# Gate and up of two feed-forward parts by seven block products, with low weight halves added by DMA

## The chip, the cores and the metric

The kernel runs on one core of one Trainium2 chip. The metric is device time of one execution in microseconds (us). The engines are called as in the profile: PE (TensorE matmul), PEld (its weight loads), DVE (VectorE), ACT (ScalarE), POOL (GpSimd) and SP (SyncE, which here issues DMAs only). PEclk in a row is the granted TensorE clock; 1.00 is the upper of its two levels, 2.4 GHz.

## What is computed

One inference step of a hybrid decoder layer for 512 prompt tokens and 32 sample tokens (544 columns, 1024 features): a half-step feed-forward part, a mixer (attention and a gated delta rule), a merge, a second half-step feed-forward part, a last norm. All data are float32. The change is in the two feed-forward parts and in how weights are prepared outside the mixer.

```
def _swiglu(x, w_gu, w_down):
    gate, up = jnp.split(x @ w_gu, 2, axis=-1)
    return (jax.nn.silu(gate) * up) @ w_down

x = x + 0.5 * _swiglu(_rms(x, norm_ffn1), w_ffn1_gu, w_ffn1_down)
h = _rms(x, norm_mix)
...                                   # mixer: h @ w_in, attention, delta rule
x = x + merged.astype(x.dtype) @ w_out
x = x + 0.5 * _swiglu(_rms(x, norm_ffn2), w_ffn2_gu, w_ffn2_down)
```

D_MODEL is 1024 and D_FF is 2816, so each part has 22 tiles of 128 gate and 128 up columns (44 in both parts), and a down projection of 22 x 8 weight tiles.

## The kernel before

**Layout and numbers.** Activations stand with features on the partitions, as tiles of 128 x 544, worked on in two halves h of 272 tokens. The kernel keeps float32 precision by splitting every operand into a high part hi (rounded to the matmul's float32r type) and a rest lo. A product of one weight tile with one half of the tokens is three matmuls of 128x128 by 128x272: hi with hi, hi with lo, lo with hi (`unit`). A unit of work over 8 weight tiles is so 24 matmuls into one PSUM bank.

**Order.** `make_plan` writes a list of units, and `kernel_units` goes through it: it brings in weights for the unit (`prefetch`), issues its matmuls, and issues what empties its bank (`evac`) one or more units later. Every engine works through its own instructions in that order. In a feed-forward part the units are, for 11 column tiles, gate and up for both halves (`u_g`, `u_u`: 4 units, 96 matmuls for a tile), then 16 down units over these 11 tiles (`u_d`), and the same again. The mixer in the middle has side chains that a meter interleaves; its order is the same on every engine before and after the change.

**Weights.** They come as chunks of 8 tiles (128 x 1024, 512 KB) by plain DMAs from SP (from POOL in the mixer) into a few raw buffers. `split_next` takes a group of 4 tiles: ACT copies it as hi into a G tile, then DVE (in the mixer POOL) writes raw - hi as lo. 12 G tiles are held in the feed-forward parts, and a look-ahead of 4 groups is kept (LA). A chunk's buffer takes its next load when both of its groups are split.

**Around them.** `xw_tile` makes hi and lo of x * w_norm; the 1/rms of the tokens (`R(h)`) is multiplied in when gate and up leave PSUM. PSUM has 8 banks: 3 called mm and 5 called sd. Nearly all instructions carry line 120 (131 after), where the meter calls the engine, so the rows are read by their tile names: xh, xl (x as hi and lo), hh (gated activations), G (weights as hi and lo), raw, r (1/rms), acc (sums of squares), H (scratch of 272 columns).

Of the kernel before, what the change touches and what calls it, by code (L numbers as in the profile page):

```python
# [25 lines left out]
FB = 11  # L26
# [11 lines left out]
CFG = dict(S=62, S2=4, G=4, G2=8, RAW=2, U3=3, H=10, HM=6, LA=4, LAG=3.0, SLACK=0.0, BANKS=3, PRE=3, LOV=("pa", "pb"), CV=0, WARM=4, EP=8, DUE=2, RES=0, RQ="gpsimd")  # L38


# [85 lines left out]
class Plan:  # L126
    """Order in which the 128 x 128 weight tiles are used; host and chip follow it."""
# [16 lines left out]
def stagger(n, tail, head=0):  # L144
    """(tile, half) order: the first `head` and the last `tail` tiles go half by half."""
    out = [(i, h) for h in range(2) for i in range(head)]
    for i in range(head, n - tail):
        out += [(i, 0), (i, 1)]
    out += [(i, h) for h in range(2) for i in range(n - tail, n)]
    return out  # L150


def make_plan():
    pl = Plan()
    units = []

    def ffn(which):
        gu, dn = f"w_ffn{which}_gu", f"w_ffn{which}_down"
        for b in range(2):
            order = stagger(FB, 0, 2 if b == 0 else 0) if (which, b) != (1, 0) else stagger(FB, 2, 2)  # L160
            for f, h in order:
                f += b * FB
                units.append(("g", which, f, h, pl.col(gu, range(KT), f * P)))
                units.append(("u", which, f, h, pl.col(gu, range(KT), (FT + f) * P)))
            for n, h in stagger(KT, 0 if b == 0 else 2 if which == 1 else 4):
                units.append(("d", which, b, n, h, pl.col(dn, range(b * FB, b * FB + FB), n * P)))

# [36 lines left out]
def consts():  # L204
    """Arrays that depend on shapes alone: identity, masks and distances."""
# [53 lines left out]
class Builder:  # L259
    def __init__(self, tc, nc, A, pl, units, cp, sp, pp, dp):  # L260
# [5 lines left out]
        self.next_group = 0  # L266
        self.next_raw = self.top = 0
        self.side = []
        self.due, self.rings = {}, {}
        self.last = False  # L270
        self.busy = set()
        self.nps = 0
        self.in_mix = False
        self.plan_groups()
# [15 lines left out]
    def until(self, ok):  # L290
        """The side chains go on until something holds."""
# [26 lines left out]
    def S2(self, i, shape=(P, NT), dt=F32, name="s2"):  # L318
        return self.T(shape, dt, "S2", CFG["S2"], name) if i < CFG["S2"] else self.S(shape, dt, name)

    def ring(self, tag, bufs, t):
        """A tile waits for the one whose place it takes."""
# [26 lines left out]
    def mm_ps(self):  # L349
        self.nps += 1  # L350
        if not self.in_mix and self.nps % 8 > 2:
            return self.sd_ps()
# [28 lines left out]
    def mm(self, out, lhsT, rhs, start=True, stop=True):  # L381
        return self.nc.tensor.matmul(out, lhsT, rhs, start=start, stop=stop)
# [5 lines left out]
    def rsqrt(self, out, v, tmp, steps):  # L388
        """out = v ** -0.5 by a shifted exponent and Newton steps."""
# [3 lines left out]
        for k in range(steps):  # L393
            a, b = (-0.703952253, 0.703952253 * 2.38924456) if k == 0 else (-0.5, 1.5)
            self.tt(tmp, out, out, ALU.mult)
            self.stt(tmp, tmp, a, v, ALU.mult, ALU.mult)
            self.stt(out, tmp, b, out, ALU.add, ALU.mult)
            yield "vector"

# [1 line left out]
    def load_raw(self, upto):  # L401
        nch = self.A["in_W_dram"].shape[0]
        while self.next_raw <= min(upto, nch - 1):
            c = self.next_raw
            pool, tag, bufs = self.sp, "raw", CFG["RAW"]
            if c % 3 == 2 and not self.in_mix and c * CHUNK // GRP not in self.resident:
                pool, tag, bufs = self.mp, "raw2", 1
# [5 lines left out]
    def plan_groups(self):  # L413
        self.last_use, self.resident = {}, set()
        first_pa = next(i for i, u in enumerate(self.units) if u[0] == "pa")
        first_ba = next(i for i, u in enumerate(self.units) if u[0] == "ba")
        for i, u in enumerate(self.units):
            for t in u[-1]:
                self.last_use[t // GRP] = i
                if first_ba <= i < first_pa:  # L420
                    self.resident.add(t // GRP)
        self.held = {"G": [], "G2": []}

    def split_next(self, ui, pool=None):
        """Bring the next group of weight tiles in as hi + lo if a slot is free."""
        k = self.next_group
        c = k * GRP // CHUNK
        for tag, bufs in (("G2", CFG["G2"]), ("G", CFG["G"])):
            if tag == "G2" and (k in self.resident or self.in_mix):
                continue  # L430
# [3 lines left out]
        else:  # L434
            return False
        self.held[tag].append(k)
        self.load_raw(c)
        o = (k * GRP % CHUNK) * P
        src = self.raws[c][:, o:o + GRP * P]
# [210 lines left out]
    def kernel_units(self):  # L650
# [4 lines left out]
        for ui, u in enumerate(self.units):  # L655
# [8 lines left out]
            for e in pend[:n]:  # L664
                e()
# [1128 lines left out]
```

## Time and profile before

| what | value |
|---|---|
| time, median of 3 runs | 1730.75 us (1727.0 to 1732.26) |
| span of the profiled execution | 1730.2 us |
| PE busy | 1656.1 us, 96% |
| DVE, ACT, POOL busy | 62%, 33%, 22% |
| DMA, mean over the span | 119 GB/s |

The profiled execution's span lies inside the three measured times; what lies around the span is no more than the spread of the runs. How to read the rows: the page's first part gives busy time by engine; its fourth part follows back what released the last work; the windows give the same busy times for one stretch, with the number of instructions, and the groups give the mean time of one instruction of a kind.

### The profile page before, as it was taken

How to read it: one execution, taken by the hardware profiler on the slowest of the kernel's cores; microseconds unless marked ns; L12 is line 12 of the kernel's file. 1: busy time of each engine (PE TensorE's matmuls, PEld its weight loads, DVE VectorE, ACT ScalarE, POOL GpSimd, SP SyncE). 2: the span in 40 equal slices, each digit the busy share in tenths (PEclk: the TensorE clock that was granted, in tenths of full speed). 3: DMA queues.
4: the chain of work that ended last, by engine and by line, in shares of the span. 5: the costliest groups of instructions: out<-in, count | busy, mean ns of one | idle time of the engine just before them, and what ended most of it. 6: DMA issues, size and time to landing. Idle time of an engine off the chain costs nothing.

```text
span 1730.2 us, 33573 instructions
## 1 busy us (share of the span) xinstructions
PE 1656.1 (96%) x13373; PEld 1607.8 (93%) x13373; DVE 1072.3 (62%) x2508; ACT 573.1 (33%) x1356; POOL 373.4 (22%) x441
## 2 busy tenths in 40 slices
PE   8999999999988999999899899999999999999997
PEld 7999999999988888888889788999999999999996
DVE  7754255545879869789958665344456654255534
ACT  5332223332332324343333244333233323223332
POOL 5000000011545534454425233420011000000012
PEclk9999999999999999999999999999999999999999
DMA  5223222322333455446347666332243222223221
GB/s 177 87 85 98 86 86 86 98 85 75 111 100 115 135 180 185 135 156 193 117 137 238 171 219 182 123 119 89 86 139 97 84 89 87 97 74 98 86 75 63
DMA packets 116434, 205.13 MB, mean 119 GB/s; under 512 B 30962, under 2 KB 57108, under 8 KB 116276
## 3 DMA queue, kind: packets, MB, share of 16 engines
q1 hardware_dynamic: 104708, 162.43, 29.2%
q0 software_dynamic: 10992, 39.99, 7.7%
q8 instruction: 105, 1.72, 0.4%
q10 hardware_dynamic: 576, 0.56, 0.1%
q14 instruction: 53, 0.43, 0.1%
HBM read 172.20 MB, written 30.73 MB: 117 GB/s over the span
## 4 chain that ended last, share of the span: by engine, by line
PE 73%; DVE 20%; DMA 3%; ACT 2%; issue 2%; SPq 1%; POOL 0%; DVEq 0%; ACTq 0%
PE sd L120 40%; PE mm L120 32%; DVE y L120 4%; DVE Yc L120 3%; DVE inv L120 2%; DVE H L120 1%; DVE nrm L120 1%; DVE ast L120 1%; DVE av L120 1%; DVE s L120 1%; DVE R L120 1%; DMA md<-ast 1%; DVE U L120 1%; DVE kq L120 1%; DVE r L120 1%
## 5 line engine op out<-in xcount | busy, mean ns | idle before, releaser
L120 PE MATMUL mm<-xh,G 128*128 128x272 f32 x3632 | 753.7, 297 | 21.6 <-DVE smp L120 10.4
L120 PEld LDWEIGHTS mm<-xh,G 128*128 128x128 f32 x3632 | 596.6, 192 | 42.5 <-issue 26.5
L120 PE MATMUL mm<-xl,G 128*128 128x272 f32 x1816 | 530.0, 292 | 0.5 <-DVE xl L120 0.4
L120 PE MATMUL sd<-xh,G 128*128 128x272 f32 x1904 | 363.4, 288 | 0.0
L120 PEld LDWEIGHTS mm<-xl,G 128*128 128x128 f32 x1816 | 349.2, 192 | 1.4 <-DVE xl L120 0.6
L120 ACT ACTIVATE G<-raw 128x512 fp32r<-128x512 f32 x474 | 273.3, 619 | 178.6 <-PE mm L120 111.6
L120 PEld LDWEIGHTS sd<-xh,G 128*128 128x128 f32 x1904 | 300.5, 188 | 0.2
L120 POOL TENSOR_TENSOR G<-raw,G 128x512 fp32r<-128x512 f32 x158 | 217.3, 1391 | 322.7 <-ACT G L120 303.0
L120 PE MATMUL sd<-xl,G 128*128 128x272 f32 x952 | 273.8, 288 | 0.0
L120 DVE TENSOR_TENSOR G<-raw,G 128x512 fp32r<-128x512 f32 x316 | 204.7, 690 | 70.9 <-ACT G L120 66.7
L120 POOL TENSOR_TENSOR acc<-acc,H 128x272 f32<-128x272 f32 x55 | 44.7, 814 | 911.5 <-ACT H L120 908.1
L120 PEld LDWEIGHTS sd<-xl,G 128*128 128x128 f32 x952 | 179.0, 188 | 0.1
L120 PE MATMUL sd<-hh,G 128*128 128x272 f32 x1287 | 163.0, 288 | 0.0
L120 PEld LDWEIGHTS sd<-hh,G 128*128 128x128 f32 x1287 | 161.8, 188 | 0.1
L120 ACT ACTIVATE H<-H 128x272 f32<-128x272 f32 (+1 forms) x105 | 45.1, 429 | 193.4 <-DVE H L120 193.4
L120 ACT ACTIVATE hh<-H 128x272 fp32r<-128x272 f32 x88 | 38.0, 431 | 202.0 <-DVE H L120 202.0
L120 PE MATMUL mm<-hh,G 128*128 128x272 f32 x825 | 104.7, 288 | 0.0
L120 PEld LDWEIGHTS mm<-hh,G 128*128 128x128 f32 x825 | 103.8, 188 | 0.0
L120 DVE SCALAR_TENSOR_TENSOR y<-U,vec,y 128x568 f32<-128x568 f32 x72 | 94.2, 1308 | 7.8 <-ACT y L120 6.0
L120 DVE SCALAR_TENSOR_TENSOR H<-H,H 128x272 f32<-128x272 f32 x120 | 55.2, 460 | 26.3 <-ACT H L120 25.8
L120 DVE SCALAR_TENSOR_TENSOR x<-sd,x 128x272 f32<-128x272 f32 x49 | 21.4, 439 | 77.9 <-PE sd L120 77.9
L120 DVE TENSOR_TENSOR hh<-H,hh 128x272 fp32r<-128x272 f32 x88 | 38.9, 442 | 43.8 <-ACT hh L120 43.8
(257 smaller groups left out, 1853.3 us busy)
## 6 DMA issues: line engine op xcount, KB each, us to landing
raw<-in_W_dram SPq DMA_DIRECT2D x161, 512.0 KB, 3.6
raw<-in_W_dram POOLq DMA_DIRECT2D x76, 512.0 KB, 4.0
qkv<-qd SPq DMA_DIRECT2D x36, 256.0 KB, 5.4
st<-in_ssm_dram SPq DMA_DIRECT2D x32, 256.0 KB, 4.5
cache<-in_kc_dram SPq DMA_DIRECT2D x28, 256.0 KB, 5.2
cache<-in_vc_dram SPq DMA_DIRECT2D x28, 256.0 KB, 4.3
qd<-av SPq DMA_DIRECT2D x24, 256.0 KB, 4.2
out_dram<-av SPq DMA_DIRECT2D x24, 256.0 KB, 3.8
```

The lines of the kernel that those rows point to most:

```text
L120: r = f(*args, **kw)
```

## The change

**Seven products.** For the last 15 of 22 column tiles in the first part and the last 16 in the second, gate and up of both halves are computed as one 2 x 2 block product: gate and up by lower and upper half of the features (4 weight tiles each), times these halves by the two halves of the tokens. Seven products of 4 weight tiles each (12 matmuls) stand in place of 8 (the table PROD). Products 1 and 2 and 4 use weights as they are (A11, A12, A22), the others use sums of weight groups (S1 to S4), which `sums` makes on DVE (on POOL for the first 3 tiles of each part) from the raw chunks into 6 new buffers sw. The activations' block sums (T1 to T4) are made once for each part by `tset`, during the last plain tiles. The first 7 and 6 column tiles stay as they were.

**Seeds.** A tile uses three banks A, B, C. B starts as a copy of -A that ACT writes into PSUM after product 1, and products 6, 7 and 4 are summed onto it. A matmul with a zero matrix (float32, 272 columns) opens the first five B banks of each part.

**Low weights.** Outside the mixer, from unit 6 on, a plain group's lo is no longer written by DVE: ACT writes -hi beside hi, and POOL issues a DMA that reads the same 256 KB again from DRAM and adds them onto -hi. lo of the sums S1 to S4 stays on DVE.

**Sizes.** 4 raw buffers (2 shared, 2 of the phase) and 11 G tiles, look-ahead 8 groups and at most 2 new groups for a unit; 3 blocks of 8, 7 and 7 column tiles instead of 2 of 11; the last 4 down tiles of both parts go half by half; the first x tiles are loaded after four raw chunks instead of one.

In the built program PE has 372 fewer matmuls of 272 columns and 10 with the zero matrix more. The core of the diff:

```diff
-CFG = dict(S=62, S2=4, G=4, G2=8, RAW=2, U3=3, H=10, HM=6, LA=4, ..., EP=8, DUE=2, RES=0, RQ="gpsimd")
+CFG = dict(S=62, G=4, G2=7, SW=6, RAW=2, RAW2=2, U3=3, H=7, HM=6, LA=4, LF=8, LS=5, EP=6, ..., DUE=3, RES=0, RQ="gpsimd")
+PROD = {1: ("A11", "B11", "A", True), 2: ("A12", "B21", "A", False), 6: ("S2", "T2", "B", False), 7: ("S3", "T3", "B", False),
+        4: ("A22", "T4", "B", False), 5: ("S1", "T1", "C", True), 3: ("S4", "B22", "C", False)}
+FBS = (8, 7, 7)
+NC = {1: 7, 2: 6}
+EARLY = 3
+TS = {1: (-20, -16, -12, -8), 2: (-18, -15, -11, -7)}
...
+        for b, n in enumerate(FBS):
+            for f in range(max(f0, nc), f0 + n + 1):
+                if f < FT:
+                    w(f, *[p for p in (1, 5) if (f, p) not in begun])
+                if f > nc and (f - 1, 3) not in begun:
+                    w(f - 1, 3)
+                if f < FT and (f, 6) not in begun:
+                    w(f, 6)
+                if f > nc and (f - 1, 4) not in begun:
+                    w(f - 1, 4)
+                if f < FT and (f, 2) not in begun:
+                    w(f, 2, 7)
+            for m, h in stagger(KT, 0 if b < 2 else 4):
+                units.append(("d", which, b, m, h, pl.col(dn, range(f0, f0 + n), m * P)))
+            f0 += n
...
+    def sums(self, j):
+        k = self.jobs[j] if j < len(self.jobs) else ()
+        if not k or k[0] == "g" or k in self.sw or self.in_mix or not self.have(k):
+            return
+        kind, gx, gy = k
+        eng = self.nc.gpsimd if gx in self.early else None
...
+        if kind == "S1":
+            self.tt(new("S1"), self.raw(gy), self.raw(gy + 1), ALU.add, eng)
...
+            self.tt(new("S2"), self.sw["S1", gx, gy], self.raw(gx), ALU.add, eng)
...
+            self.tt(new("S3"), self.raw(gx), self.raw(gy + 1), ALU.add, eng)
+            self.tt(new("S4"), self.raw(gx + 1), self.sw["S2", gx, gy], ALU.add, eng)
+        self.read_raw(k)
+        self.load_raws()
...
         self.act(t[:, 0, :], src, AF.Copy)
-        self.tt(t[:, 1, :], src, t[:, 0, :], ALU.subtract, self.nc.gpsimd if pool else None)
+        if raw and not self.in_mix and ui >= CFG["EP"]:
+            self.act(t[:, 1, :], t[:, 0, :], AF.Copy, scale=-1.0)
+            self.read_raw(k)
+            self.load_raws()
+            self.nc.gpsimd.dma_start(t[:, 1, :], self.A["in_W_dram"][...][:, o:o + GRP * P], accum_op=ALU.add)
...
-        load_x(0, range(4))
-        self.load_raw(0)
-        load_x(0, range(4, KT))
+        load_x(0, range(4))
+        self.load_raws()
+        load_x(0, range(4, KT))
...
+    def u_w(self, which, f, p, wids):
+        wn, bn, bank, start = PROD[p]
+        if start:
+            self.bank[f, bank] = self.mm_ps(bank)[:, :NH]
+        ps = self.bank[f, bank]
+        hi, lo = self.w(wids[0])
+        for j in range(4):
+            c = slice(j * P, j * P + P)
+            xh, xl = self.ts_bs[bn, j, 0], self.ts_bs[bn, j, 1]
+            self.mm(ps, hi[:, c], xh, start and j == 0, False, True)
+            self.mm(ps, hi[:, c], xl, False, False, True)
+            self.mm(ps, lo[:, c], xh, False, j == 3 and last, True)
...
+            if p == 1:
+                b = self.bank[f, "B"] = self.mm_ps("B")[:, :NH]
+                if self.nb < 5:
+                    self.mm(b, self.zero, self.x[0][:, h0], True, True, True)
+                self.act(b, ps, AF.Copy, scale=-1.0)
+            elif p == 6:
+                self.act(e["V"], ps, AF.Copy)
+            elif p == 5:
+                self.act(e["p5"], ps, AF.Copy)
+            elif p == 2:
+                self.act(e["t"][:, h0], ps, AF.Tanh, scale=0.5)
+            elif p == 7:
+                self.tt(e["u"], ps, e.pop("p5"), ALU.subtract)
+                self.stt(t, t, 1.0, self.bank.pop((f, "A")), ALU.add, ALU.mult)
+            elif p == 3:
+                self.tt(g, ps, g, ALU.subtract)
+                self.act(t, g, AF.Tanh, scale=0.5)
+                self.stt(t, t, 1.0, g, ALU.add, ALU.mult)
+                self.tt(t, t, e.pop("u"), ALU.mult)
+            else:
+                self.tt(t[:, h0], t[:, h0], ps, ALU.mult)
+                self.split(*self.h[f], t)
```

ACT in the first part, at one column tile, before. hh is a gated activation's hi, H is its tanh, G<-raw a weight group's hi:

```order
L120 ACTIVATE hh_216_1547<-H_211_1511 128x272
L120 ACTIVATE G_218_1554<-raw_198_1384 128x512
L120 ACTIVATE G_219_1557<-raw_198_1384 128x512
L120 ACTIVATE H_223_1588<-H_222_1587 128x272
L120 ACTIVATE G_224_1591<-raw_208_1483 128x512
L120 ACTIVATE G_225_1594<-raw_208_1483 128x512
L120 ACTIVATE hh_228_1624<-H_223_1588 128x272
L120 ACTIVATE H_232_1657<-H_231_1656 128x272
```

ACT in the first part, among the tiles with seven products, after. t<-mm is product 2's tanh, sd<-mm is the seed of B, H<-sd the copy of product 5, G<-sw a sum's hi, G<-G a -hi:

```order
L131 ACTIVATE hh_389_2630<-t_370_2509 128x544
L131 ACTIVATE G_391_2635<-raw_363_2454 128x512
L131 ACTIVATE G_391_2635<-G_391_2635 128x512
L131 ACTIVATE t_392_2651<-mm_372_2513 128x272
L131 ACTIVATE G_393_2653<-sw_383_2591 128x512
L131 ACTIVATE G_398_2676<-sw_375_2532 128x512
L131 ACTIVATE sd_400_2691<-mm_394_2655 128x272
L131 ACTIVATE G_401_2694<-sw_387_2613 128x512
L131 ACTIVATE H_402_2708<-sd_399_2678 128x272
L131 ACTIVATE G_403_2711<-raw_360_2430 128x512
L131 ACTIVATE G_403_2711<-G_403_2711 128x512
L131 ACTIVATE t_392_2651<-H_386_2611 128x272
```

Where four group copies stood for a column tile there are now ten copies of 512 columns and six of 272 or 544; the next chunk, raw_404, takes the buffer of raw_360, so SP issues it behind the copy G_403<-raw_360.

DVE in the first part, at one column tile, before. G<-raw is a group's lo, r is 1/rms:

```order
L120 TENSOR_TENSOR G_293_2434<-raw_279_2247,G_293_2434 128x512
L120 TENSOR_TENSOR G_294_2437<-raw_279_2247,G_294_2437 128x512
L120 SCALAR_TENSOR_TENSOR H_292_2431<-H_292_2431,H_291_2430 128x272
L120 TENSOR_TENSOR H_292_2431<-H_292_2431,r_73_361 128x272
L120 TENSOR_TENSOR H_292_2431<-H_292_2431,mm_296_2442 128x272
L120 TENSOR_TENSOR hh_298_2468<-H_292_2431,hh_297_2467 128x272
```

DVE in the first part, among the tiles with seven products, after, around the sum that reads raw_404 (S1, then S2); t<-t,sd is the multiplication by product 4's bank that the next hh waits for:

```order
L131 TENSOR_TENSOR sw_396_2672<-raw_363_2454,raw_382_2572 128x512
L131 TENSOR_TENSOR sw_397_2674<-raw_363_2454,sw_387_2613 128x512
L131 TENSOR_TENSOR G_398_2676<-sw_375_2532,G_398_2676 128x512
L131 TENSOR_TENSOR G_401_2694<-sw_387_2613,G_401_2694 128x512
L131 TENSOR_TENSOR H_386_2611<-sd_377_2536,H_386_2611 128x272
L131 SCALAR_TENSOR_TENSOR t_392_2651<-t_392_2651,H_386_2611 128x272
L131 TENSOR_TENSOR t_392_2651<-t_392_2651,H_395_2668 128x272
L131 TENSOR_TENSOR sw_405_2733<-raw_404_2714 128x512
L131 TENSOR_TENSOR sw_409_2755<-sw_405_2733,raw_385_2596 128x512
L131 TENSOR_TENSOR t_392_2651<-t_392_2651,sd_378_2549 128x272
L131 TENSOR_TENSOR hh_412_2773<-t_392_2651,hh_411_2772 128x544
```

The lo of plain groups has left DVE; sums of chunks have come, and the sum of a chunk just loaded stands ahead of the multiplication that gives the tile's activations.

## Rows read from the trace of the kernel before

**Rows 1.** The page: busy time of each engine.
```profile
PE 1656.1 (96%) x13373; PEld 1607.8 (93%) x13373; DVE 1072.3 (62%) x2508; ACT 573.1 (33%) x1356; POOL 373.4 (22%) x441
```

**Rows 2.** The page: chain that ended last, by engine.
```profile
PE 73%; DVE 20%; DMA 3%; ACT 2%; issue 2%; SPq 1%; POOL 0%; DVEq 0%; ACTq 0%
```

**Rows 3.** Windows, inside the two feed-forward parts; columns as in the first row.
```profile
core 0: us, PE busy (x) PEld busy (x) DVE busy (x) ACT busy (x) POOL busy (x), PEclk, DMA share, GB/s
100.00:370.00 270.00, 270.00 (x2159) 270.00 (x2159) 135.79 (x271) 79.51 (x161) 1.55 (x2) 1.00 0.28 87
1340.00:1690.00 350.00, 350.00 (x2791) 350.00 (x2790) 176.44 (x354) 108.85 (x221) 5.41 (x7) 1.00 0.27 88
```

**Rows 4.** Waits of PE, 0 to 380 us: in total, times, longest.
```profile
PE mm L120 <- DVE H L120: 3.3, 2, 2.5
PE sd L120 <- ACT H L120: 2.3, 1, 2.3
PE mm L120 <- ACT G L120: 1.8, 1, 1.8
```

**Rows 5.** Timeline at the end: start us, us, engine, operation.
```profile
1703.57 0.62 PE L120 MATMUL sd<-acc,mats 128*128 128x272 f32 x2
1703.82 4.48 PE L120 MATMUL sd<-hh,G 128*128 128x272 f32 x33
```

**Rows 6.** Groups by form: x count, busy us, mean ns of one, idle before.
```profile
L120 ACT ACTIVATE G<-raw 128x512 fp32r<-128x512 f32 x474 | 273.3, 619 | 178.6 <-PE mm L120 111.6 <-PE sd L120 43.7 <-DMA raw<-in_W_dram 12.1
L120 POOL TENSOR_TENSOR G<-raw,G 128x512 fp32r<-128x512 f32 x158 | 217.3, 1391 | 322.7 <-ACT G L120 303.0 <-PE sd L120 19.3
L120 DVE TENSOR_TENSOR G<-raw,G 128x512 fp32r<-128x512 f32 x316 | 204.7, 690 | 70.9 <-ACT G L120 66.7
...
L120 ACT ACTIVATE H<-H 128x272 f32<-128x272 f32 x104 | 44.9, 431 | 193.4 <-DVE H L120 193.4
...
L120 DVE TENSOR_TENSOR hh<-H,hh 128x272 fp32r<-128x272 f32 x88 | 38.9, 442 | 43.8 <-ACT hh L120 43.8
```

**Rows 7.** DMA issues, 100 to 370 us: KB each, median us to landing.
```profile
raw<-in_W_dram SPq DMA_DIRECT2D x45, 512.0 KB, 3.6
```

**Rows 8.** Windows of the later mixer and the merge.
```profile
700.00:900.00 200.00, 187.37 (x1624) 174.85 (x1626) 162.81 (x451) 75.61 (x224) 86.03 (x107) 0.98 0.48 152
900.00:1100.00 200.00, 185.69 (x1553) 169.93 (x1542) 130.54 (x367) 71.35 (x188) 78.50 (x87) 0.97 0.62 189
1100.00:1300.00 200.00, 199.83 (x1609) 198.92 (x1608) 93.46 (x190) 67.65 (x146) 27.59 (x29) 1.00 0.35 113
```

**Rows 9.** DMA issues: 700 to 900, 900 to 1100, then (two rows) 1100 to 1300 us.
```profile
raw<-in_W_dram POOLq DMA_DIRECT2D x19, 512.0 KB, 4.2
raw<-in_W_dram POOLq DMA_DIRECT2D x20, 512.0 KB, 5.1
raw<-in_W_dram SPq DMA_DIRECT2D x26, 512.0 KB, 3.5
raw<-in_W_dram POOLq DMA_DIRECT2D x8, 512.0 KB, 3.9
```

**Rows 10.** The page: packets, MB, share of 16 engines of POOL's DMA queue.
```profile
q0 software_dynamic: 10992, 39.99, 7.7%
```

**Rows 11.** Windows of the start.
```profile
0.00:20.00 20.00, 15.91 (x90) 14.20 (x91) 11.66 (x17) 14.97 (x34) 9.73 (x14) 1.00 0.81 277
20.00:100.00 80.00, 75.66 (x576) 74.44 (x576) 58.32 (x112) 26.88 (x60) 12.70 (x13) 0.96 0.29 92
```

**Rows 12.** Timeline, 24 to 36 us: DVE beside POOL.
```profile
25.96 0.42 DVE L120 TENSOR_SCALAR H<-sd 128x272 f32<-128x272 f32 x1
...
27.57 5.68 POOL L120 TENSOR_TENSOR G<-raw,G 128x512 fp32r<-128x512 f32 x4
27.88 1.34 DVE L120 TENSOR_TENSOR H<-r 128x272 f32<-128x272 f32 x1
```

More of the change, by code (lines that the diff above doesn't have):

```diff
@@ L25 @@
 FT = 22
-FB = 11
 EPS = 1e-6
@@ L379, in act, with mm @@
         return self.nc.scalar.activation(out, a, f, **kw)
-    def mm(self, out, lhsT, rhs, start=True, stop=True):
-        return self.nc.tensor.matmul(out, lhsT, rhs, start=start, stop=stop)
+    def mm(self, out, lhsT, rhs, start=True, stop=True, part=False):
+        kw = {"skip_group_check": True} if part else {}
+        return self.nc.tensor.matmul(out, lhsT, rhs, start=start, stop=stop, **kw)
     def tr(self, out, a):
@@ L411, in load_raw, with read_raw @@
             self.next_raw += 1
[L413 to L422, printed above, removed]
+    def read_raw(self, k):
+        gs, per = self.chunks(k)
+        for g in gs:
+            c = g // per
+            self.reads[c] -= 1
+            if not self.reads[c]:
+                del self.raws[c]
+                for live in self.raw_live.values():
+                    live.discard(c)
@@ L435, in split_next @@
             return False
+        self.load_raws()
+        for i in range(j, j + CFG["LS"]):
+            self.sums(i)
+        if not (self.have(k) if raw else k in self.sw):
+            return False
         self.held[tag].append(k)
-        self.load_raw(c)
-        o = (k * GRP % CHUNK) * P
-        src = self.raws[c][:, o:o + GRP * P]
+        src = self.raw(k[1]) if raw else self.sw[k]
         mem = self.mp if tag == "G2" else self.sp
@@ L508, in build @@
         self.acc, self.r = [None, None], [None, None]
-        self.xn = [(self.S(dt=F32R, name="xh"), self.S(dt=F32R, name="xl")) for _ in range(KT)]
+        self.bset_new()
         def seq(f, h, after):
@@ L651, in kernel_units @@
         nu = len(self.units)
-        self.h = {}
-        self.gsum = {}
+        first = {w: next(i for i, u in enumerate(self.units) if u[0] == "w" and u[1] == w) for w in (1, 2)}
+        self.tsets = {first[w] + TS[w][j]: (w, j) for w in (1, 2) for j in range(4)}
+        self.h, self.ev, self.bank = {}, {}, {}
         pend = []
@@ L663, in kernel_units @@
             n = 4 if ui == 3 else len(pend)
+            if u[0] in "wd" and ui + 1 < nu and self.units[ui + 1][0] == u[0]:
+                n -= 1
             for e in pend[:n]:
@@ L666, in kernel_units @@
             pend = pend[n:]
+            for f in self.late:
+                f()
+            self.late = []
+            if ui in self.tsets:
+                self.do_los()
+                w, j = self.tsets[ui]
+                self.tset(j, 2 * w - 2)
             self.pump()
@@ L1682, in evac @@
             if h == 0:
-                self.m.append(tuple(self.S2(2 * n + k, dt=F32R, name="mh") for k in range(2)))
+                self.m.append(tuple(self.S(dt=F32R, name="mh") for k in range(2)))
             hi, lo = self.m[n]
```

296 lines of the change are left out of this document (231 added, 65 removed).

## The prediction

> **What bounds the kernel now.** I read the page's busy times first: PE is busy for 96% of the span, no other engine for more than 62% [rows 1]. The chain that ended last lies on PE for 73% and on DVE for 20% [rows 2]. The change stays out of the mixer (its order is the same on every engine), so what counts is the windows inside the two feed-forward parts. There PE never stops: 270.0 us busy of 270.0 with 2159 matmuls, 350.0 of 350.0 with 2791 [rows 3]. That is 0.125 us for a matmul of 272 columns, with the clock at its upper level (1.00). DVE is busy for half of these windows, ACT for 30%, the DMA engines for 28%. PE's waits in the first part are 7.4 us, all near the start [rows 4]. So a matmul removed there is worth 0.125 us, as long as nothing else becomes late.
>
> **What is removed.** 31 tiles by 96 - 84 = 12 matmuls are 372, times 0.125: **-46.5 us**. The DVE work removed was under PE and gives nothing by itself.
>
> **What PE gets in addition.** Ten matmuls with the zero matrix in float32. The nearest row is a norm's float32 matmul of the same 272 columns: its records start at 1703.57 and the next matmul starts at 1703.82 [rows 5], 0.25 us; with a short wait behind it 0.4. Ten cost 2.5 to 4: **+3**.
>
> **ACT and DVE among the seven-product tiles.** A tile is 84 matmuls, 10.5 us. ACT has ten copies of 512 columns at 0.62, five passes over 272 at 0.43, and one over 544 (no row; between 0.62 and 0.86, by its columns 0.64) [rows 6]: 9.0 us. DVE has eight operations of 512 at 0.69, six of 272 at 0.44 and one of 544 (0.73): 8.9. Both fit by their sums, with 85% of PE's time, where they had 30 and 50%. Among down and plain units a group of 4 weight tiles lasts 24 matmuls, 3.0 us, and ACT has 1.24 for it: hidden. The merge gets some 50 of these -hi copies, 31 us beside 68 busy of 200 [rows 8]: hidden too.
>
> **The wait that is added.** Order matters more than sums. As the rows of ACT and DVE in the section on the change show, the buffer of a tile's second chunk comes free with the copy of its A22, and the next chunk loaded there is read at once by the sum S1. DVE waits in S1 for that DMA; behind it in its queue are S2 and the multiplication by product 4; ACT's hh waits for this, and behind hh on ACT stand nine operations that end with the next A22. This closes a ring, one turn for a tile: S1, S2 and the multiplication 0.69 + 0.69 + 0.44 = 1.8; hh 0.64; six copies of 512 (3.7) and three passes of 272 (1.3), less some 0.2 since neighbours on ACT overlap; together 7.25 us and the landing of 512 KB. Landing took 3.6 us in the feed-forward part [rows 7], where the turn is 10.85. It grows with load: POOL's loads took 4.2 at a DMA share of 0.48 and 5.1 at 0.62 [rows 8, 9], and SP's take 0.4 less than POOL's in the one window that has both (3.5 and 3.9 [rows 9]). A tile now loads 1.05 MB and reads 0.79 MB again. 87 GB/s at a share of 0.28 are 311 GB/s for a full share [rows 3], and POOL's queue moved 40 MB in 7.7% of 1730 us, 300 GB/s [rows 10]. If an added byte costs what a plain one does, that is 5.9 us of 10.5, a share of 0.56, and SP's landing between 3.8 and 4.7: I take 4.2, the middle. The turn is 11.45, 0.95 more than PE needs. ACT's seed stands in this ring, and product 6 waits for it, so PE takes the ring's pace once it has lost its lead. The program's order has such turns in the long runs of product tiles alone: 4 and 3 in each part, 14. The lead (the seed has about 0.7 us to spare in each of four runs) takes 3: 14 x 0.95 - 3 = 10.3, **+11**. At 3.6 it is 14 x 0.35 - 3, about 2; at 5.1, 14 x 1.85 - 3 = 23; I keep 0 and 36 (a landing of 6, as far above 5.1 as that above 4.2) as ends.
>
> **The low halves by DMA.** hi, -hi, POOL's issue and the DMA are some 0.6 + 0.6 + 0.6 + 4 = 6 us, and the look-ahead of 8 groups is 12 us in the shortest units: hidden, at nothing, while DMA keeps up. POOL's queue holds hardly anything else but 24 early sums of 1.4 us [rows 6].
>
> **Ends of runs, start, tail.** At six places a run of product tiles ends and down units need its last activations: product 3's passes, then product 4's, some 4 us on DVE and ACT against 3.7 us of matmuls ahead of the first use; with a late DVE more. +0.7 each, **+4** (0 to 10). At the end the half-by-half down units are 21 matmuls instead of 33, so the first half's norm and stores on DVE no longer end ahead of PE: **+1** (0 to 2). At the start, where 666 records stand in 100 us instead of some 800 [rows 11], four x tiles are now queued behind 2 MB of weights instead of 0.5 MB: 1.5 MB at 277 GB/s is 5.4 us, of which PE's early units hide about 2. Against it, four low halves leave POOL; beside them DVE's operation of 272 columns took 1.34 us instead of 0.42 [rows 12], in a chain of six that PE waits for. I set the start at **0** (-4 to +4). The Trainium skill, "SBUF — State Buffer", section "Who interferes with whom", says that a DVE instruction with two SBUF inputs contends with a GpSimd instruction that reads SBUF; rows 12 agree. By it the 24 early sums on POOL slow DVE again; this is left in the ends.
>
> **The sum.** -46.5 + 3 + 11 + 4 + 1 + 0 = -27.5. The profiled span is 1730.2 and the median 1730.75, so I make no difference between them: **1703 us**.
>
> **Rivals.** *Full gain.* The chunks land in time (3.6 us or less) and the ends of runs cost little: -46.5 + 3 + 1 with 2 for the ring, 1690. For it: the DMA engines were at 28% and neither ACT nor DVE is full. Against it: the ring is 0.35 too long even then. *Crowded loads.* The adding transfers take their time from the raw loads and the landing goes to 5.1 to 6: the ring costs 23 to 36, so 1715 to 1728. The Trainium skill, "Collectives: The Full Stack", section "The bandwidth ceiling: the fold count and why AG ≠ RS ≠ AR", says that a DMA which adds reads two sources and so halves the rate; no run here shows it yet. By that rule the share is (3.4 + 2 x 2.5) of 10.5, 0.8, and this rival is the one that follows. *DMA bound, slower than before.* It is decided by what an added byte costs against a plain one, k. A group of 256 KB outside the product tiles takes 0.84(1 + k) us against 3.0 of matmuls, a product tile 3.4 + 2.5k against 10.5. From k = 2.8 on the 183 groups outside lose as much as the rest gains; at k = 3 they lose 0.37 each, 68, and the tiles 14, which gives 1730 - 38.5 + 82 = 1774. Nothing in the trace shows an adding DMA; against it, POOL's plain ones run at the full rate [rows 10]. *No gain.* DVE or ACT lags by its order in more places than the ring (product 4's bank, the sums on POOL), and 40 us of small stalls eat it all: 1730. Against it, the windows have 15% of slack left on both engines.
>
> **How the numbers follow.** Forecast (1695 to 1714): 0.52. Full gain (1685 to 1695): 0.18. Crowded loads (1714 to 1728): 0.14. No gain (1725 to 1736): 0.05. DMA bound: 0.11. The range goes from 1686 to 1728 and holds the first three but for their edges, some 0.82. A change of under 0.3%, 5.2 us, is about what a measurement of this kernel can't tell from none. Faster by more: 0.52 + 0.18 + 0.12 = 0.82. Within 0.3%: 0.05. Slower: 0.13.
>
> **What the profile will show.** Right: records of the two parts down by 372 less some for the zero matmuls, windows inside plain and down units still at 0.125 us a matmul, and short waits of PE for ACT's seeds (sd) in the runs of product tiles, DVE's sums waiting for raw DMAs of 4 to 5 us. Full gain: PE without a gap in these runs. Crowded loads: landings above 5 us and a share near 0.8. DMA bound: PE waits for G tiles whose last writer is POOL's DMA, in down units too. What would make it wrong in kind: PE waits that have neither the seeds nor the chunks behind them.

## The result

The changed kernel takes 1743.85 us (1740.53 to 1748.94) where the kernel before took 1730.62 beside it: a ratio of 1.0073, interval 1.0047 to 1.0099. It is slower; the forecast was 1703. The profiled execution's span went from 1730.2 to 1738.8 us; it is the shortest of the changed kernel's four, so the account below is of its 8.6 us.

The page of the changed kernel: busy time, instructions; POOL's DMA queue; the adding DMAs from issue to landing. They answer to [rows 1, 10].

```profile
PE 1628.5 (94%) x13021; PEld 1576.8 (91%) x13021; DVE 1053.9 (61%) x2446; ACT 828.1 (48%) x1815; POOL 638.4 (37%) x737
q0 software_dynamic: 50880, 112.88, 32.8%
G<-in_W_dram POOLq DMA_DIRECT2D x276, 256.0 KB, 6.9
```

PE has 352 records fewer and 28 us less work, so the matmuls are gone; yet the span grew. PE must now stand still where it did not. Windows show where. First the kernel before, then the changed one (columns as in [rows 3]):

```profile
0.00:70.00 70.00, 61.58 (x424) 58.63 (x425) 50.84 (x89) 30.84 (x69) 22.43 (x26) 0.95 0.42 139
70.00:160.00 90.00, 90.00 (x721) 90.00 (x720) 51.89 (x106) 31.40 (x65) 0.00 (x0) 1.00 0.29 89
160.00:370.00 210.00, 210.00 (x1680) 210.00 (x1679) 103.03 (x205) 59.12 (x119) 1.55 (x2) 1.00 0.28 89
1140.00:1200.00 60.00, 59.83 (x478) 59.61 (x477) 34.20 (x71) 20.10 (x42) 4.75 (x6) 1.00 0.34 106
1380.00:1450.00 70.00, 70.00 (x560) 70.00 (x558) 40.66 (x83) 22.17 (x47) 0.00 (x0) 1.00 0.29 91
```

```profile
0.00:70.00 70.00, 58.87 (x401) 55.95 (x402) 50.84 (x97) 38.77 (x83) 22.89 (x30) 0.90 0.64 176
70.00:160.00 90.00, 77.69 (x574) 76.78 (x573) 50.35 (x82) 48.68 (x94) 32.14 (x33) 0.91 0.68 155
160.00:370.00 210.00, 210.00 (x1672) 209.72 (x1671) 115.93 (x216) 129.32 (x252) 57.13 (x65) 1.00 0.73 164
1140.00:1200.00 60.00, 56.42 (x435) 55.66 (x434) 22.55 (x53) 31.20 (x60) 22.32 (x25) 0.97 0.79 199
1380.00:1450.00 70.00, 58.09 (x439) 57.29 (x438) 41.64 (x65) 41.48 (x83) 29.34 (x29) 0.90 0.59 134
```

A full window holds 8.0 PE records per us (1680 in 210). So the change loses 23 records (2.9 us) at the start, **147 (18 us) from 70 to 160**, 8 (1 us) in the long stretch of product tiles and down units, 43 (5.4 us) where the merge begins, **121 (15 us) from 1380 to 1450**. The end adds 5.6 us: from the start of the last down unit's last matmul to the end 13.9 us before and 19.5 after. That is 48 us lost against 352 x 0.125 = 44 gained (372 matmuls less the ten with zeros, which have two records each); some 4 us more are lost from 370 to 1140 and from 1450 to 1690 (18 records each). The two large losses are one place in the program, the *entry*: the last ordinary tiles and the first products of each feed-forward part. PE's waits in these stretches (60 to 160, 1370 to 1440, 1690 to the end):

```profile
PE sd L131 <- ACT sd L131: 7.7, 1, 7.7
PE mm L131 <- DVE H L131: 4.4, 1, 4.4
...
PE sd L131 <- ACT sd L131: 10.7, 1, 10.7
...
PE sd L131 <- POOL acc L131: 6.0, 1, 6.0
```

The first product waits for an mm bank that DVE has still to empty, then product 6 waits for ACT's first seed, which stands on ACT behind the evacuations of the last ordinary tiles. The timeline of the first entry (PE, then ACT, then DVE) shows how late these are:

```profile
103.81 2.18 PE L131 MATMUL sd<-bs,G 128*128 128x272 f32 x16
110.42 3.06 PE L131 MATMUL mm<-bs,G 128*128 128x272 f32 x12 [4.44 <-DVE H L131]
124.42 3.09 PE L131 MATMUL sd<-bs,G 128*128 128x272 f32 x12 [7.72 <-ACT sd L131]
...
123.98 0.38 ACT L131 ACTIVATE sd<-mm 128x272 f32<-128x272 f32 x1
...
93.29 3.40 DVE L131 TENSOR_TENSOR hh<-H,hh 128x272 fp32r<-128x272 f32 x1 [0.50 <-ACT hh L131]
104.46 0.44 DVE L131 TENSOR_TENSOR hh<-H,hh 128x272 fp32r<-128x272 f32 x1 [1.49 <-ACT hh L131]
113.11 3.60 DVE L131 TENSOR_TENSOR G<-sw,G 128x512 fp32r<-128x512 f32 x1
117.57 0.44 DVE L131 TENSOR_TENSOR H<-H,mm 128x272 f32<-128x272 f32 x1
```

PE is through with the last ordinary unit at 106.0; DVE takes "up" of the last tile's first half out of its bank at 117.57 only. Two DVE operations that take 0.44 and 0.69 us elsewhere took 3.40 and 3.60 here; POOL made its early sums beside them, two in a row each time (timeline of POOL):

```profile
93.50 1.64 POOL L131 TENSOR_TENSOR sw<-raw,raw 128x512 f32<-128x512 f32 x1
94.75 1.63 POOL L131 TENSOR_TENSOR sw<-raw,sw 128x512 f32<-128x512 f32 x1
...
113.33 1.60 POOL L131 TENSOR_TENSOR sw<-raw,raw 128x512 f32<-128x512 f32 x1
114.57 1.58 POOL L131 TENSOR_TENSOR sw<-raw,sw 128x512 f32<-128x512 f32 x1
```
The waits are also paid twice: after each, the first 12 matmuls took 3.06 and 3.09 us, 0.25 each against 0.125 before. The granted clock was 0.50 there, the lower level (window of the first):

```profile
110.40:113.40 3.00, 2.98 (x13) 3.00 (x14) 2.63 (x3) 2.19 (x5) 2.79 (x4) 0.50 0.78 203
```

### The profile page after: what moved, and what is told of

It reads as the page before. It is cut to its first block, busy times and chain, and to the rows that moved or that the text cites. A ratio compares the mean times of both kernels' runs of the same rounds, so it can differ in the third digit from the quotient of the medians.

```text
span 1738.8 us, 33775 instructions
## 1 busy us (share of the span) xinstructions
PE 1628.5 (94%) x13021; PEld 1576.8 (91%) x13021; DVE 1053.9 (61%) x2446; ACT 828.1 (48%) x1815; POOL 638.4 (37%) x737
## 5 line engine op out<-in xcount | busy, mean ns | idle before, releaser
L131 PE MATMUL mm<-xh,G 128*128 128x272 f32 x2560 | 545.5, 300 | 19.5 <-DVE smp L131 10.4
L131 PEld LDWEIGHTS mm<-xh,G 128*128 128x128 f32 x2560 | 425.3, 193 | 38.2 <-issue 25.6
L131 POOL DMA_DIRECT2D G<-in_W_dram x276 | 240.9, 873 | 594.6 <-ACT G L131 298.6
L131 PE MATMUL mm<-xl,G 128*128 128x272 f32 x1280 | 375.1, 293 | 0.3
L131 PE MATMUL sd<-bs,G 128*128 128x272 f32 x2628 | 349.2, 291 | 20.3 <-ACT sd L131 19.1
L131 PEld LDWEIGHTS sd<-bs,G 128*128 128x128 f32 x2628 | 338.3, 190 | 22.9 <-ACT sd L131 20.4
L131 PEld LDWEIGHTS mm<-xl,G 128*128 128x128 f32 x1280 | 247.3, 193 | 1.5 <-DVE xl L131 0.7
L131 PE MATMUL mm<-bs,G 128*128 128x272 f32 x1224 | 173.6, 297 | 9.2 <-DVE H L131 4.4
L131 ACT ACTIVATE G<-G 128x512 fp32r<-128x512 f32 x276 | 174.5, 632 | 8.7
L131 PEld LDWEIGHTS mm<-bs,G 128*128 128x128 f32 x1224 | 165.3, 196 | 11.5 <-ACT G L131 7.7
```

The lines of the kernel that those rows point to most:

```text
L131: r = f(*args, **kw)
```

## The experiments

Not all runs were on the same chip; the kernel before took 1735 to 1738 us beside those below, so ratios to it are compared. The table counts PE records at the entries, by the windows above (lost against the kernel before at 8.0 per us), with the ratio and its interval. Each count is from one profile; e7 and e8, which are the same program (see below), differ by 22 records, 2.8 us, so a difference of 3 us between two rows may be none. c2 is the changed kernel with four edits, given in the last part of this section; e10 to e15 and e18 build on it.

| kernel | 70-160 | lost us | 1380-1450 | lost us | ratio |
|---|---|---|---|---|---|
| before | 721 | | 560 | | 1 |
| changed kernel | 574 | 18 | 439 | 15 | 1.0073 (1.0047-1.0099) |
| e1 sums on DVE | 602 | 15 | 466 | 12 | 1.0021 (0.9999-1.0042) |
| e6 same, spare adds on POOL | 574 | 18 | 442 | 15 | 1.0055 (1.0034-1.0076) |
| e9 sets earlier | 571 | 19 | 488 | 9 | 1.0033 (1.0016-1.0050) |
| e7 no low halves of sets | 683 | 5 | 544 | 2 | 0.9869 (0.9834-0.9904) |
| e8 the same program as e7 | 705 | 2 | 544 | 2 | 0.9884 (0.9847-0.9922) |
| c2 four edits | 622 | 12 | 474 | 11 | 0.9958 (0.9938-0.9978) |
| e10 c2, set lows by DMA | 548 | 22 | 437 | 15 | 1.0021 (1.0001-1.0040) |
| e12 c2, late set lows by DMA | 597 | 16 | 466 | 12 | 0.9984 (0.9968-1.0001) |
| e13 control: c2, fewer buffers | 601 | 15 | 458 | 13 | 1.0014 (0.9999-1.0029) |
| **e13 own tiles** | 676 | 6 | 538 | 3 | **0.9912 (0.9883-0.9940)** |
| e14 own tiles, earlier entry | 627 | 12 | 428 | 17 | 1.0011 (0.9993-1.0029) |
| e15 own tiles, set lows by DMA | 671 | 6 | 518 | 5 | 0.9961 (0.9940-0.9981) |
| e16 changed kernel, own tiles | 630 | 11 | 466 | 12 | 1.0020 (0.9996-1.0043) |
| e18 c2, own tiles, other room | 704 | 2 | 549 | 1 | 0.9993 (0.9974-1.0012) |

### POOL's sums beside DVE

```diff
-EARLY = 3
+EARLY = 0
```

> The changed kernel with all block sums on VectorE (EARLY = 0), none on GpSimd; nothing else is changed. Theory 1 (GpSimd's sums beside VectorE's operations on two SBUF operands lengthen those, and the first products wait): the excess of VectorE's operations of 11.3 us (45-160) and 13.2 us (1320-1430) disappears, the two entries lose under 6 us each instead of 18 and 15, and the time falls from 1744 to about 1720 (1712 to 1728). Theory 2 (VectorE has too much to do at the entries, the sums' engine does not matter): 12 sums per entry of 0.69 us put 8.3 us on VectorE, which is already busy 17 us of 20 there, the entries lose as much or more, and the time is 1744 to 1760.

e6 adds, where POOL's sums were, POOL additions of a constant tile:

> As the run with all sums on VectorE, but GpSimd issues, at the places of its former sums, additions of the same size of a constant tile to itself into a tile that nobody reads: nothing waits for GpSimd's results, and only the meeting of the two engines at SBUF is left. Theory 1 (contention): VectorE's operations at the entries are lengthened again to 2 to 3.6 us, and the time stands near the changed kernel's, 1735 to 1750. Rival (the first products waited for GpSimd's slow sums of 1.4 us themselves, not for a lengthened VectorE): the time is that of the run with all sums on VectorE, within 3 us.

e1 gave 0.5% back, and each entry 3 us: theory 1's mechanism, but not its size. In its timeline the two kinds of operation are back at 0.44 and 0.68:

```profile
110.01 0.44 DVE L131 TENSOR_TENSOR hh<-H,hh 128x272 fp32r<-128x272 f32 x1 [0.50 <-ACT hh L131]
111.32 0.68 DVE L131 TENSOR_TENSOR G<-sw,G 128x512 fp32r<-128x512 f32 x1
```

e6 lost two thirds of that again although nothing waits for the results of POOL's additions: DVE's operations at the entries were longer by up to 1.0 us each, not the 2 to 3.6 us expected. (POOL issues adding DMAs behind the additions; from 60 to 160 us PE waits for one once, 1.6 us, and 1.1 in e1.) So the meeting of the two engines costs some 6 us in all, and POOL's results are not what is waited for. 27 us of loss remain in e1, and something else holds the entries.

### DVE's work, or the pool's tiles?

e9 shifts the sets (TS) by 2 units; e7 deletes the line of `tset` that subtracts the low halves, so the products read the high half twice; e8 takes no tile for them either.

> As the run with all sums on VectorE, but the four operand sets of the products are made 2 units (6 us) earlier: at 22, 18, 14 and 10 units ahead of the first product in the first FFN instead of 20, 16, 12 and 8, and 20, 17, 13, 9 instead of 18, 15, 11, 7 in the second. Theory 1 (VectorE's queue is too full just ahead of the products): 6 us of its work leave the last 25 us, and each entry loses 3 to 6 us less, 1730 to 1735. Theory 2 (waits for tiles of the common pool): earlier sets take their tiles while the old operands still hold theirs, the waits grow, and the time is 1741 or more.

> As the run with all sums on VectorE, but the low halves of the operand sets that the products read are not made: 14 subtractions of 0.72 us at each entry are gone from VectorE (their tiles are still taken from the pool), and the products read the high half twice, so the output is not that of the reference; TensorE's instructions are the same. Theory 1 (at the entries VectorE's queue holds more than it can do: the evacuations of the last ordinary tiles stand behind operand sets and sums, and the first product's bank waits for them): 10 us less work there, each entry loses under 6 us instead of 15 and 12, and the time is 1.2% under that of the run with all sums on VectorE, about 1722. Theory 2 (the evacuations wait for tiles of the common pool that TensorE still reads): the waits stay, the entries lose 10 us or more each, and the time falls by under 0.3%.

> As the run without the low halves of the products' operand sets, and their 14 tiles of the common pool of 62 are not taken either, so that nothing at the entries waits for a tile that TensorE still reads; the output is not that of the reference for the same reason. Theory 1 (VectorE's work alone): the same time as the run that keeps the tiles, within 3 us. Theory 2 (waits for tiles of the pool): 10 to 20 us under the run that keeps the tiles, with the entries losing under 5 us each only here.

e7 and e8 are 1.5 and 1.4% under e1, but they do not tell the theories apart: the builder drops tiles that nothing writes, so e7 had given up the 14 tiles as well, and the two built programs are the same, instruction for instruction. e9 tells more: sets made earlier did not help as a whole (the first entry lost 4 us more than in e1, the second 3 less), and its first entry shows a new wait on DVE (78 to 126 us):

```profile
DVE bs L131 <- PE sd L131: 9.1, 1, 9.1
```

DVE there waits to *write* an operand of PE until PE has done something. The program of the changed kernel says what (its order on ACT and DVE at this place, with the semaphores waited for; PE_49 counts what PE has finished):

```
117 L131 ACTIVATE hh_203_1130<-H_188_1076 128x272 [waits DVE_49,PE_49]
139 L131 TENSOR_TENSOR hh_204_1131<-H_188_1076,hh_203_1130 128x272 [waits PE_49,Activation_49]
140 L131 TENSOR_TENSOR bs_193_1090<-xw_189_1080,bs_192_1089 128x544 [waits PE_49]
```

hh_203 is made from H and read by PE later: its PE wait can only be for its place. In the built program that place was held by bs_19, an operand of the ordinary tiles, and the wait is for the matmul of the last ordinary unit that reads bs_19 last. The common pool has 62 tiles (S), and at the entry all are held: 8 of x, 16 of the old operands, 24 of the sets made so far, 4 of the set's scratch, 10 of h. The last set's four low halves and the next h take the places of the old operands, which PE reads to the end of the last ordinary unit. DVE and ACT stop there, in their order, with the evacuations of earlier units behind them; and PE, through with its last unit, waits for those.

e10 and e12 (on c2) take the work from DVE and leave the tiles (the diff is e10's; e12 does it for the last two sets):

```diff
-        self.late += [lambda src=src, d=d: self.tt(d[1], src, d[0], ALU.subtract) for src, d in out]
+        for src, d in out:
+            self.act(d[1], d[0], AF.Copy, scale=-1.0)
+            self.nc.gpsimd.dma_start(d[1], src, accum_op=ALU.add)
```

> The run with four edits, and the 14 low halves of the products' operand sets at each entry made as the change makes low weights: an ACT copy of -hi and a DMA that adds the f32 tile onto it, instead of a subtraction of 0.72 us on VectorE. Theory (VectorE's queue at the entries was too full): 10 us of work leave VectorE there as in the run that left the halves out, the entries lose about 5 and 3 us instead of 12 and 11, and the time is 0.8 to 1.1% under the run with four edits, 1711 to 1716. Rival (the 14 copies of 0.64 us make ScalarE late, or 14 adding DMAs of 278 KB at once crowd the weights' DMAs): no gain, 1727 to 1740.

> As the run with the operand sets' low halves by adding DMAs, but only for the last two of the four sets of each entry (8 of 14 tiles: VectorE keeps the first six). Theory: the load of VectorE's last 25 us ahead of the products decides, so most of the gain stays, within 4 us of the run with all 14 by DMA. Rival (the late DMAs, not the early ones, make the products wait): 4 us or more above it.

With 10 us less on DVE the first entry of e10 lost 10 us *more* and the second 4. The wait for the place moved to ACT, and DVE behind it did nothing for 9.5 us (e10, waits of ACT and DVE, 78 to 126 us; then PE's, 60 to 160):

```profile
ACT bs L131 <- PE sd L131: 5.7, 1, 5.7
...
DVE hh L131 <- ACT hh L131: 14.2, 6, 9.5
```

```profile
PE sd L131 <- ACT sd L131: 4.3, 1, 4.3
PE mm L131 <- DMA G<-in_W_dram: 3.9, 1, 3.9
PE mm L131 <- DVE H L131: 3.9, 1, 3.9
PE sd L131 <- DMA G<-in_W_dram: 1.3, 1, 1.3
```

PE's waits for the bank and the seed, 8.2 us, are hardly less than c2's 8.8, so less work on DVE did not shorten them. What came on top is the rival's: 5.2 us for adding DMAs, and 7.3 us at the second entry, where the seed's wait did fall, from 8.2 to 3.9. So e10 speaks against theory 1 at the first entry alone, and does not show what a place costs. e12 is 6 us under e10 and 0.3% over c2, which neither expectation had.

Then the opposite, the same work without the waits. Six tiles of their own for the last set's four low halves and one column tile's h (hi and lo), paid for with other buffers, and a control that only pays:

```diff
-            out.append((src, [self.S(dt=F32R, name="bs") for _ in range(2)]))
+            lo = self.T([P, NT], F32R, "own", 6) if j == 3 else self.S(dt=F32R, name="bs")
+            out.append((src, [self.S(dt=F32R, name="bs"), lo]))
...
+                new = (lambda: self.T([P, NT], F32R, "own", 6)) if f == NC[which] - 2 else (lambda: self.S(dt=F32R, name="hh"))
-CFG = dict(... G2=7, SW=6, ... H=7 ...)
+CFG = dict(... G2=5, SW=5, ... H=5 ...)
```

> The run with four edits, with six tiles of their own for the last operand set's four low halves and the second last ordinary tile's two halves of h, so that nothing at either entry takes the place of a tile that TensorE still reads; VectorE's work is the same. The room comes from fewer buffers: 5 instead of 7 for split weights, 5 instead of 6 for sums, 5 instead of 7 for half tiles. Theory 2 (VectorE and ScalarE stood behind writes that waited for the last ordinary units to read the old operands): the entries lose about 5 us each instead of 12 and 11, 1714 to 1720. Theory 1 (VectorE's work alone): the entries lose as before, 1727 to 1735.

> The run with four edits with the same fewer buffers (5, 5 and 5 instead of 7, 6 and 7) and no tiles of their own: the price of the buffers. Both theories: the time of the run with four edits or up to 8 us more, 1729 to 1738.

The control's waits (ACT, then DVE, 78 to 126 us), and its window beside that of own tiles:

```profile
ACT hh L131 <- PE sd L131: 7.9, 1, 7.9
...
DVE hh L131 <- PE sd L131: 9.0, 1, 9.0
...
70.00:160.00 90.00, 80.56 (x601) 79.56 (x600) 41.01 (x85) 43.03 (x80) 20.77 (x24) 0.92 0.67 148
```

```profile
70.00:160.00 90.00, 86.40 (x676) 85.97 (x675) 44.38 (x91) 45.72 (x84) 22.49 (x26) 0.98 0.72 161
```

With own tiles no wait of ACT or DVE to write an operand or h is left there; PE's waits fall from 9.4 to 3.6 us, DVE is no less busy. 1.0% is between the two, 17.8 us: theory 2. This is the worth of the places where buffers are few: in c2 itself the waits to write an h are shorter (DVE 3.1, ACT 1.5 us), and e13 gains 0.5% on c2, the fewer buffers paid. Two further runs bound it.

> As the run with four edits, with products for 33 tiles instead of 31 (6 and 5 ordinary tiles instead of 7 and 6, which hold two tiles of the pool each), own tiles for the last set's four low halves, the sets made at 18, 15, 12, 9 and 14, 12, 10, 8 units ahead, and 6, 5, 5 buffers instead of 7, 6, 7: also without a wait for a tile that TensorE reads. Theory 2: the entries lose about 5 us each and 24 matmuls (3 us) are gone too, 1711 to 1718. Theory 1 (VectorE's work, now in a shorter time ahead of the products): the entries lose 12 us or more each, 1727 or more.

> The run with own tiles, and the 14 low halves of each entry's operand sets by ACT copies of -hi and adding DMAs, which without own tiles cost 9 us more than VectorE's subtractions. Theory 2 with nothing of theory 1: no better than the run with own tiles (within 4 us, or worse by the DMAs that compete with the weights'). Theory 1 on top of theory 2 (VectorE's 10 us per entry count once nothing waits for tiles): 5 to 10 us under the run with own tiles.

e14 went as theory 1 said: without such waits, but with the sets crowded into less time, the entries lost 12 and 17 us, to late seeds (4.8, 6.5 us) and weight DMAs (2.0, 4.6). So DVE's and ACT's work seems to count too once its time is cut. With its time as it was, less of it gave nothing: e15 is 0.5% over e13. But PE waits 4.5 us for adding DMAs at e15's second entry, so this is no clean test.

Last, own tiles in the changed kernel itself, POOL's sums kept:

> The changed kernel with GpSimd's early sums as they are and the six own tiles (and 5, 5, 5 buffers) of the run with own tiles; nothing else is changed. If the waits for tiles of the pool alone make the entries' loss, it falls to about 6 us each and the time is 1.2% under the changed kernel's, 0.996 of the kernel before. If the two delays lie beside each other (the lengthened VectorE operations reach the evacuations as late as the pool's tiles come free, so that taking one away uncovers the other), the entries still lose 10 us or more each and the time stays within 8 us of the changed kernel's, 1.002 to 1.007 of the kernel before.

It gives 0.5% back, as taking away POOL's sums did, and the entries still lose 11 and 12 us, as in the second expectation; both together, with the rest of c2, leave 8 of 33 us (e13). That the two delays lie partly beside each other in the changed kernel would explain why its trace shows DVE late, and hardly a wait for places, but it is not shown. Apart, sums on DVE, own tiles and c2's other edits take away 7, 10 and 4 us, 21 of the 25 that they take together, and e16 pays for fewer buffers as well (0.6% from c2 to the control), which no run of the changed kernel has by themselves.

### The adding DMAs

e5 is the kernel before with low halves by adding DMAs and nothing else; e4 the products with all lows on DVE.

> The kernel before (all matmuls, no products) with the low weights outside the mixer made by an ACT copy of -hi and a DMA that adds the raw weights onto it. Theory (the adding DMAs are hidden in the FFN, where TensorE stays full, and cost 5 us at the merge's start, where the DMA share reaches 1.0): 1736 (1729 to 1740). Rival (the adding DMA's 7 us landing and its second reading of the weights cost in the FFN too, at each group): up to 1760, with TensorE below 160 matmuls per 20 us in the FFN.

> The changed kernel with all low weights by subtractions on VectorE (GpSimd's path as in the mixer), no adding DMA; the block products are as in the change. Theory (VectorE cannot hold sums, lows and evacuations of a tile: 8.9 us + 3 subtractions of 0.69 us = 11.0 us against 10.5 us of matmuls per tile): 1750 to 1760, with VectorE over 0.95 busy in the product runs. Rival (the adding DMAs are what costs): about 1710.

e5: 1.0164 (1.0118-1.0210), worse than either expectation. Windows of e5: in the long stretch PE is full; the loss sits where a part begins (and at the merge, 450 records from 1140 to 1200 instead of 478).

```profile
40.00:60.00 20.00, 16.02 (x117) 15.80 (x117) 12.42 (x30) 8.55 (x18) 3.45 (x4) 0.93 0.32 70
160.00:370.00 210.00, 210.00 (x1680) 210.00 (x1679) 58.35 (x133) 103.37 (x189) 59.71 (x69) 1.00 0.79 172
1340.00:1360.00 20.00, 14.13 (x95) 13.73 (x94) 11.25 (x27) 11.03 (x21) 6.69 (x8) 0.83 0.67 157
```

e4: 1.0400 (1.0359-1.0442), over twice the expected loss, and not by a full DVE: it was busy 122 us of the 210, where PE lost 206 records.

```profile
160.00:370.00 210.00, 193.64 (x1474) 191.22 (x1473) 122.27 (x227) 73.47 (x151) 5.86 (x4) 0.97 0.24 76
```

Its waits there (DVE, then PE) are those of the forecast's ring:

```profile
DVE sw L131 <- DMA raw<-in_W_dram: 34.7, 11, 3.9
...
PE sd L131 <- ACT sd L131: 15.2, 7, 3.1
```

In e4 a chunk's buffer takes its next load only behind DVE's subtraction, which makes the ring's turn longer although the landing is 3.5 us. So the products need their low halves made elsewhere, because of DVE's order rather than its sum; no run moves the load alone. And the adding DMAs are no free replacement: they cost at beginnings. Whether e5's smaller look-ahead (4 groups, 8 in the change) is why its loss is larger there was not tried.

### Four edits, and the room for own tiles

c2: EARLY = 0; lows on DVE from the merge to the second part; `FBS = (7, 7, 8)`; x tiles ahead of the first weights.

> Four edits in four places of the time, read apart by stage: all sums on VectorE (as in the run of that name); low weights by VectorE from the merge to the second FFN; last blocks of 7, 7, 8 tiles instead of 8, 7, 7, so that the last down units have 24 matmuls instead of 21; and the second four tiles of x loaded ahead of the first weights. Theory: the merge's start loses no matmuls at 1160 to 1180 (5 us back), the tail from the last matmul to the end falls from 19.6 to about 17 us, the first 100 us give back 2 us, the entries stay as in the run with all sums on VectorE: together 10 us below that run, 1728 to 1734. Rival (VectorE becomes the wait in the merge, where it is busy 13 of 20 us with its old lows): no gain there, 1735 to 1740.

The merge's start is full again (1140 to 1200):

```profile
1140.00:1200.00 60.00, 59.84 (x478) 59.62 (x477) 35.15 (x74) 22.29 (x46) 6.76 (x7) 1.00 0.41 132
```

and the first 70 us hold 423 records instead of 401; the end fell from 19.5 to 18.8 only, not to 17.

> As the run with own tiles (four edits), with their room taken from the split weights' buffers alone: 4 instead of 7, with 6 for sums and 7 half tiles as in the change. If half tiles and sums are what the stretches outside the entries lack, the first 70 us give back 3 us and the time is 2 to 5 us under the run with own tiles, 1714 to 1717; if the split weights' look-ahead is, TensorE waits for weights in the product runs and the time is 1720 to 1730.

The entries are nearly free in e18 (2 and 1 us), but the first 70 us gave nothing back (380 records, 397 in e13), and from 160 to 370 it has 1603 records instead of 1662. PE's longest waits in total there (160 to 440) and in the second part (1460 to 1720) are the seeds, not weights:

```profile
PE sd L131 <- ACT sd L131: 5.3, 7, 0.9
...
PE sd L131 <- ACT sd L131: 6.4, 8, 1.0
```

e13, at 0.9912, beats both kernels.

## Why the prediction was wrong

**The step that failed** is one that the sum did not have: what it takes to *enter* the product runs. The forecast costed a tile in the steady run, the ends of runs, the start and the tail; the 28 tiles of the operand sets were counted neither as work nor as places in the pool. The slowing of DVE by the early sums on POOL, which it knew of, it left "in the ends" without a price. Measured: 33 us at the two entries. Own tiles and sums on DVE, with c2's other edits, take 25 of them away; alone, sums on DVE take 7 and own tiles 10 (with fewer buffers). How much of the loss is due to each in the changed kernel, and what the last 8 us are, stays open. No rival had this mechanism; "no gain" came nearest, but it looked for small stalls, and these are two large ones. The forecast's own test caught it: a PE wait that has neither the seeds nor the chunks behind it (the mm bank, 4.4 us), ahead of the only long seed waits, one at each entry.

**Right.** The matmuls removed: -352 records, with 0.125 us each in the full stretches. ACT and DVE in the steady run fit (340 to 360 us: PE full with 162, DVE 15.30 and ACT 16.68 of 20, where the sums gave 16.9 and 17.1). The zero matmuls are cheap: from 190 to 244 us the three product tiles with one took 10.97 us each and the next two 10.53, which for ten is 4.4 where the sum had 3. The start lost 2.9 us, inside its -4 to +4.

**Mis-sized: the ring, +11.** It is there: from 190 to 265 us DVE waits five times for raw chunks, 8.1 us in all. But its landing was put too high. The chunks that DVE waits for landed 3.4 to 4.3 us after their issue, as these two do (SP's issue, then DVE's sum):

```profile
228.83 0.33 SPq L131 DMA_DIRECT2D raw<-in_W_dram  x1
232.21 0.69 DVE L131 TENSOR_TENSOR sw<-raw 128x512 f32<-128x512 f32 x1 [1.47 <-DMA raw<-in_W_dram]
...
239.36 0.33 SPq L131 DMA_DIRECT2D raw<-in_W_dram  x1
243.64 0.69 DVE L131 TENSOR_TENSOR sw<-raw 128x512 f32<-128x512 f32 x1 [2.08 <-DMA raw<-in_W_dram]
```

At 3.6 the forecast itself gave 2, and PE's waits for seeds in the product runs are 0.7 us (1460 to 1720; none from 130 to 380). SP's median from 100 to 370 was 5.9, but DVE did not wait for the chunks that raise it. So what the rival of crowded loads rests on was seen, a share of 0.78 (200 to 240 us) and landings above 5 us, and its price of 23 to 36 us was not. Where the ring is longer (e4) or split weights have fewer buffers (e18, which differs from e13 in its buffers alone), the seed waits that were forecast are there.

**Too high: the ends of runs, +4.** PE's waits for hh, from 130 to 380 and from 1416 to 1720 us, are 0.8 us in all.

**Wrong: the low halves at nothing.** Adding DMAs took 7.0 us from issue, not 4, and the merge's start lost 5.4 us (3.4 of them a wait of PE for one such DMA), which c2 gave back. DMA rows of the changed kernel, 100 to 370 us:

```profile
q0 software_dynamic: 10792, 19.66, 43.8%
q1 hardware_dynamic: 6607, 24.08, 27.8%
...
raw<-in_W_dram SPq DMA_DIRECT2D x47, 512.0 KB, 5.9
G<-in_W_dram POOLq DMA_DIRECT2D x79, 256.0 KB, 7.0
```

POOL's queue moved 19.66 MB in 43.8% of 270 us. That is 166 GB/s for a full share against 311 [rows 3] (SP's plain loads beside them: 321): an added byte costs 1.9 plain ones. That stays below the k = 2.8 from which the forecast's DMA-bound rival would have decided. The Trainium skill, "Collectives: The Full Stack", section "The bandwidth ceiling: the fold count and why AG ≠ RS ≠ AR", says of a ReduceScatter that its add needs two source reads and so halves the rate; the 1.9 here agrees.

**Too low: the tail, +1.** Measured 5.6. Down units of 21 matmuls let PE finish its last unit at 1719.5, while DVE, in its order, works at the first half's norm and products until 1721.8 and only then takes up the last four tiles of x; PE's last sums wait 6.0 us for POOL's acc behind that. Units of 24 matmuls (c2) gave 0.7 back.

**A reading.** PE's waits before the change were 8.4 us from 0 to 380, not 7.4 ([rows 4] leave one of 1.0 out); nothing rests on it.

## What to carry to other kernels

When a change sets up new operands while old ones are still in use, count the places in their pool at that moment, tile by tile: an engine whose order holds a write into a place that PE still reads stops, and takes the evacuations behind it along. The order of a program shows such a wait before it has run, as a semaphore of the reader on an instruction that reads nothing of it. Look at each change of regime by itself, since a full steady state says nothing of its entry, and test one cause with the other's work kept: leaving work out also left out its tiles.

## What was not expected of the hardware

DVE operations of 0.44 and 0.69 us took 3.40 and 3.60 beside POOL's additions: they lasted until two additions of 1.6 us, back to back, had ended, though DVE's records start 0.2 us ahead of POOL's first (93.29 and 93.50, 113.11 and 113.33). The Trainium skill, "SBUF — State Buffer", section "Who interferes with whom", names this pair, and the trace agrees. A byte of an adding DMA from DRAM cost 1.9 plain ones, and 256 KB landed after 6.9 us. And stalls of 4.4 and 7.7 us were paid with the clock as well: the granted clock was 0.50 behind each, with 12 matmuls in 3.06 us instead of 1.5, and 0.91 over the window from 70 to 160 us where it had been 1.00.
